# Attention of a two-block layer on one core: items head by head, value products three chunks behind, three ways out of PSUM

## The chip, the cores and the metric

The kernel runs on 1 core of a Trainium2 chip. The metric is the device time of one execution in microseconds; the time given is the median of several executions. Engines are named as in the profile: PE (TensorE matmul) and PEld (its weight loads), DVE (VectorE), ACT (ScalarE), POOL (GpSimd), SP (the queue that issues the transfers).

## The reference, cut to what matters

Two blocks are computed on 1024 tokens of width 1024, all in float32. The first block mixes gated linear attention and stick-breaking attention. The second block runs two causal attentions of 8 heads each, then a gated merge, an output projection and a feed-forward layer with a convolution. The change touches the two attentions of the second block alone:

```python
def one_block(args):                  # latent attention ("attB"), query blocks of 128
    sc = (einsum('bqhd,bshd->bhqs', qn, k_nope) + einsum('bqhd,bsd->bhqs', qr, k_rope)) * scale
    sc = where(causal, sc, -inf)
    p = softmax(sc, axis=-1)
    o = einsum('bhqs,bshd->bqhd', p, v)
...
def one_block(args):                  # indexed sparse attention ("attA"): only the 256 best keys
    ...
    sc = einsum('bqgrd,bqkgd->bqgrk', qg, ksel) * scale
    sc = where(valid, sc, -inf)
    p = softmax(sc, axis=-1)
    o = einsum('bqgrk,bqkgd->bqgrd', p, vsel)
```

In the kernel the sparse attention is computed as a dense one with a mask of the selected keys, which an earlier stage writes to DRAM.

## The kernel before, in words

Precision: a float32 operand of a matmul is split into a rounded part (`hi`, the chip's fp32r type) and a rest (`lo = x - hi`), and each product is made of two or three matmuls with these parts.

`attend` (L1576 and after) runs both attentions as one list of 64 items. A pair is two heads; there are 4 pairs of attB and then 4 of attA. An item is (pair, `tp`, `h`): one head `h` and two query tiles `t = 2*tp + w` of 128 queries, in the order `tp` = 3, 0, 2, 1, so that items have 4, 1, 3 and 2 chunks of 256 keys. Causal tiles see `(t+1)*128` keys.

- `stage_a(i, w)` makes the scores of one query tile: matmuls into one of two PSUM score tiles (`ps2`, named `pb` in the trace; L1785 to L1787 for attB, L1842 and L1843 for attA), for tiles without a mask tile one more matmul that adds the causal bias (L1630), then one DVE pass that copies the scores to an SBUF tile of the `g4` ring and takes the row minimum (L1638, or L1640 with the mask), then the exponential with its row sum on ACT (L1641). The row sums go to a small tile `l`.
- `stage_c(i, c)` transposes one chunk of 256 keys of both query tiles on PE (L217) into a PSUM tile `ps` (512 columns, 384 in the last chunk of an item; two such tiles rotate). ACT copies it to `hi` (L1657), DVE subtracts to get `lo` (L1658). Both land in SBUF tiles of the ring `pt`.
- `stage_d(i, c)` multiplies the values with `hi` and `lo` (L1674), accumulating in PSUM: `pg` for head 0, `po` for head 1.
- `finish(pair, h, bank)` follows when two items (`tp` 3 and 0, or 2 and 1) of a head are complete: ACT copies one half of the accumulator (L1687), DVE adds the other half (L1689); after head 1, the reciprocals of the row sums (L1693) are spread over a PSUM tile `ps` by matmuls (L1697), ACT copies that to SBUF (L1700) and POOL multiplies (L1701).
- `setup` runs one step of a list that prepares the next pair: transfers of queries, keys and values, transposes and splits of queries and keys (`split_T`, L1741 and L1742), splits of the values on POOL (`split_v`, L1728 and L1729).

The loop at the end of `attend` writes the work out with scores two items ahead of the products (`lag = 2`), up to two chunks transposed before the first product of the item. Not this text alone sets the order on the engines: a planner (`schedule_with_timeline_sim`, L2105) orders the instructions of every engine by a simulated timeline, with the written order as priority, and adds the waits. Each engine then runs its own queue in that order. Buffers are rings (`bufs`): a tile that is asked for waits until the oldest user of its slot is done. Before the change the stage has `g4` 8, `mb` (mask tiles) 4, `pt` 6, `r2` 3.

Of the kernel before, what the change touches and what calls it, by code (L numbers as in the profile page):

```python
# [15 lines left out]
P = 128  # L16
# [138 lines left out]
class K:  # L155
# [1434 lines left out]
    def attend(self, jobs, begun, fill):  # L1590
# [8 lines left out]
        items = [(pair, tp, h) for pair in range(4 * len(jobs)) for tp in order for h in range(2)]  # L1599
# [14 lines left out]
        def stage_a(i, w):  # L1614
# [7 lines left out]
            if h == 0:  # L1622
                live["b", pair, t] = bias(t)
# [9 lines left out]
            if (place, h, w) == (1, 0, 1):  # L1633
                live["l", pair, bank] = self.col(8, "l")
            l = live["l", pair, bank]
            j = (place * 2 + w) * 2 + h
# [12 lines left out]
        def stage_c(i, c):  # L1649
            job(items[i][0])  # L1650
            pt, n = self.ps(), 0
            for s, ws in tiles(i, c):
                for w in ws:
                    self.tr(pt[:, n:n + P], live["p", i, w][:, s * P:(s + 1) * P])
                    n += P
            hi, lo = [self.tq.tile([P, 512], F32R, tag="pt", name=self.nm("pt"), bufs=self.bufs["pt"]) for _ in range(2)]
            nc.scalar.copy(hi[:, :n], pt[:, :n])  # L1657
            nc.vector.tensor_tensor(lo[:, :n], pt[:, :n], hi[:, :n], op=OP.subtract)  # L1658
            live["pt", i, c] = hi, lo

        def stage_d(i, c):
# [3 lines left out]
            if place == 1 and c == 0:  # L1665
                live["po", h] = self.po() if h else self.pg()
            po, n = live["po", h], 0
# [12 lines left out]
        def finish(pair, h, bank):  # L1680

            oT, po = job(pair)[5], live.pop(("po", h))
            q = slice(1, 3) if bank else slice(0, 4, 3)
            o = oT[:, pair % 4].rearrange("p (q t) -> p q t", q=4)[:, q]
            hs, other = slice(64 * h, 64 * h + 64), slice(64 - 64 * h, 128 - 64 * h)
            t1 = self.r2()
            nc.scalar.copy(t1[hs], po[other])  # L1687
            q2 = lambda y: y.rearrange("p (q t) -> p q t", q=2)
            nc.vector.tensor_tensor(o[hs], q2(po)[hs], q2(t1)[hs], op=OP.add)  # L1689
            if h == 0:  # L1690
                return
            rl = self.col(8, "rl")
            nc.vector.reciprocal(rl, live.pop(("l", pair, bank)))  # L1693
            pr = self.ps()
            for j in range(8):
                hh = j % 2
                nc.tensor.matmul(pr[64 * hh:64 * hh + 64, j // 2 * P:(j // 2 + 1) * P],  # L1697
                                 rl[:, j:j + 1].to_broadcast([P, 64]), self.ident, start=True, stop=True)
            R = self.r2()
            nc.scalar.copy(R, pr)  # L1700
            nc.gpsimd.tensor_tensor(o, o, q2(R), op=OP.mult)  # L1701

        lag = 2
        for k in range(len(items) + lag):
            a, i = k < len(items), k - lag
            nch = self.nk(2 * items[i][1] + 1) // 256 if i >= 0 else 0
            if a:
                stage_a(k, 1)
            if fill:
                fill.pop(0)()  # L1710
            for c in range(min(nch, 2)):
                stage_c(i, c)
            if a:
                stage_a(k, 0)
            for c in range(nch):
                stage_d(i, c)
                if c + 2 < nch:
                    stage_c(i, c + 2)
            if k % 8 >= 1:
                setup()  # L1720

# [22 lines left out]
    def block2_b(self):  # L1744
# [4 lines left out]
        def prep(pair):  # L1749
# [11 lines left out]
            def load(h):  # L1761
                if pair and h == 0:
                    load_v()
# [13 lines left out]
            if pair == 0:  # L1777
                steps.append(load_v)
# [236 lines left out]
    def block2_front(self, first):  # L2015

        pool, causal = self.tc.tile_pool, self.causal
        with pool(name=self.nm("kp2"), bufs=1, reuse_waits="tile") as self.kp2:
# [25 lines left out]
            self.bufs = {"g4": 8, "mb": 4, "pt": 6, "r2": 3}  # L2044
# [64 lines left out]
```

## Time and profile before

| | us |
|---|---|
| median of 3 runs | 2475.01 (2467.51 to 2495.38) |
| profiled execution | 2476.42 |
| its span, first to last instruction | 2474.5 |
| PE busy in the span | 2312.6 (93%) |
| PEld busy | 1900.2 (77%) |
| DVE busy | 1452.8 (59%) |
| ACT busy | 873.0 (35%) |
| POOL busy | 884.1 (36%) |

Busy time is the time in which an engine has at least one instruction running. PE's matmuls are pipelined and their ends are modelled, so one that is shown as busy can still be behind its best pace; PEld shows the weight loads that come before every matmul. The idle time of an instruction is what its engine stood still before it, with the instruction whose end released it behind the arrow. The two attentions of the second block lie between about 1222 and 1552 us of the span.

### The profile page before, as it was taken

To read this page: it belongs to the slowest core of one execution; us is meant where nothing else is said; L and a number is where in the kernel's file an instruction comes from. 1 tells how busy PE (TensorE), PEld (TensorE's weight loads), DVE (VectorE), ACT (ScalarE), POOL (GpSimd) and SP (SyncE) were. 2 spreads that over 40 slices of the span, in tenths; PEclk is the share of its full clock that TensorE was granted. 3 is DMA by queue.
4 is the path that set the end of the run, shared out by engine and by line. 5 is a ranking of instruction groups with operands and counts; after the bars stand their busy time and mean duration, and the time that the engine had idled before them with its cause. 6 is when DMAs were issued, how large, how long until landed. Compare 5 with 4: busy or idle time off the path is not lost.

```text
span 2474.5 us, 30964 instructions
## 1 busy us (share of the span) xinstructions
PE 2312.6 (93%) x12073; PEld 1900.2 (77%) x12073; DVE 1452.8 (59%) x2189; ACT 873.0 (35%) x1389; POOL 884.1 (36%) x641
## 2 busy tenths in 40 slices
PE   4999999998798999788999998899999999999997
PEld 3788887776577888667788877788888888888886
DVE  8564457668656467999777776544433333333335
ACT  4454442443314345542376776212311111111111
POOL 5211135455466353435311010631343434443341
PEclk9999999899699999899999999999999999999999
DMA  6222122222332122344511210341111111111112
GB/s 243 98 98 100 73 90 89 79 77 91 137 111 100 65 81 101 142 111 125 161 48 39 75 34 19 119 162 35 68 43 48 47 52 52 51 52 43 52 43 79
DMA packets 116415, 206.09 MB, mean 83 GB/s; under 512 B 45458, under 2 KB 67106, under 8 KB 115874
## 3 DMA queue, kind: packets, MB, share of 16 engines
q1 hardware_dynamic: 116258, 204.01, 24.0%
q8 instruction: 97, 1.59, 0.3%
q14 instruction: 60, 0.49, 0.1%
HBM read 154.14 MB, written 49.84 MB: 82 GB/s over the span
## 4 chain that ended last, share of the span: by engine, by line
PE 43%; DVE 3%; ACT 3%; issue 1%; POOL 1%; DMA 0%; SPq 0%; POOLq 0%; DVEq 0%; ACTq 0%
PE up_pb L1935 5%; PE up_pb L1936 5%; PE up_pb L1934 5%; PE br_ps L1880 3%; PE dn_ps L1989 3%; PE dn_ps L1991 3%; PE dn_ps L1990 3%; PE dn_pb L1934 1%; PE dn_pb L1936 1%; PE dn_pb L1935 1%; PE op_ps L1087 1%; PE op_ps L1085 1%; PE op_ps L1086 1%; PE attB_ps L217 1%; PE attA_po L1674 1%
## 5 line engine op out<-in xcount | busy, mean ns | idle before, releaser
L1993 DVE TENSOR_TENSOR br_h<-br_h,dn_ps 128x512 f32<-128x512 f32 x176 | 119.6, 686 | 237.6 <-PE dn_ps L1991 237.3
L1972 DVE SCALAR_TENSOR_TENSOR ffn_ws<-up_pb,cols,ffn_ws 128x1023 f32<-128x1023 f32 x66 | 84.6, 1281 | 138.9 <-ACT ffn_ws L1970 138.1
L205 POOL TENSOR_SCALAR up_wh<-up_raw 128x1024 fp32r<-128x1024 f32 x41 | 43.6, 1063 | 272.9 <-PE up_pb L1935 134.0
L1970 ACT ACTIVATE ffn_ws<-up_pb,cols 128x1024 f32<-128x1024 f32 x33 | 40.0, 1212 | 234.9 <-PE up_pb L1936 234.9
L210 POOL TENSOR_TENSOR up_wl<-up_raw,up_wh 128x1024 fp32r<-128x1024 f32 x41 | 98.4, 2401 | 20.5 <-PE up_pb L1936 17.8
L210 POOL TENSOR_TENSOR sb_wl<-sb_raw,sb_wh 128x1024 fp32r<-128x1024 f32 x15 | 37.9, 2533 | 189.6 <-ACT sb_wh L209 189.4
L1934 PE MATMUL up_pb<-br_h,up_wh 128*128 128x512 f32 x264 | 102.7, 389 | 0.0
L1935 PE MATMUL up_pb<-br_h,up_wh 128*128 128x512 f32 x264 | 102.7, 389 | 0.0
L1936 PE MATMUL up_pb<-br_h,up_wl 128*128 128x512 f32 x264 | 102.7, 389 | 0.0
L1934 PE MATMUL up_pb<-op_fh,up_wh 128*128 128x512 f32 x264 | 102.7, 389 | 0.0
L1935 PE MATMUL up_pb<-op_fl,up_wh 128*128 128x512 f32 x264 | 102.7, 389 | 0.0
L1936 PE MATMUL up_pb<-op_fh,up_wl 128*128 128x512 f32 x264 | 102.7, 389 | 0.0
L1548 ACT ACTIVATE topk_r<-topk_r 128x640 bf16<-128x640 bf16 (+1 forms) x64 | 57.4, 898 | 120.3 <-DVE topk_r L1547 120.3
L1977 ACT CAST up_g<-ffn_ws 128x1024 fp32r<-128x1024 f32 x22 | 23.1, 1049 | 176.1 <-PE dn_ps L1990 97.7
L1989 PE MATMUL dn_ps<-dn_wh,up_g 128*128 128x512 f32 x192 | 75.2, 392 | 1.3 <-DVE br_h L1993 1.3
L1990 PE MATMUL dn_ps<-dn_wl,up_g 128*128 128x512 f32 x192 | 74.8, 389 | 0.0
L1991 PE MATMUL dn_ps<-dn_wh,up_g 128*128 128x512 f32 x192 | 74.7, 389 | 0.0
L654 PE MATMUL gla_pb<-QB,gla_X 128*128 128x128 f32 x448 | 66.7, 305 | 8.4 <-DVE QB L641 7.6
L242 PE MATMUL v_ps<-sb_wh,init_hh 128*128 128x256 f32 x256 | 74.3, 291 | 0.0
L244 PE MATMUL v_ps<-sb_wh,init_hl 128*128 128x256 f32 x256 | 74.0, 289 | 0.0
L243 PE MATMUL v_ps<-sb_wl,init_hh 128*128 128x256 f32 x256 | 73.8, 288 | 0.0
L654 PEld LDWEIGHTS gla_pb<-QB,gla_X 128*128 128x128 f32 x448 | 61.5, 214 | 12.9 <-issue 4.1
(745 smaller groups left out, 7471.9 us busy)
## 6 DMA issues: line engine op xcount, KB each, us to landing
up_raw<-in_wu SPq DMA_DIRECT2D x43, 512.0 KB, 3.4
dn_raw<-in_wu SPq DMA_DIRECT2D x21, 512.0 KB, 3.5
sb_sp<-F_st SPq DMA_DIRECT2D x32, 256.0 KB, 2.0
sb_raw<-in_wu SPq DMA_DIRECT2D x15, 512.0 KB, 4.3
init_X<-in_wada SPq DMA_DIRECT2D x13, 512.0 KB, 4.4
c_raw<-in_wu SPq DMA_DIRECT2D x13, 512.0 KB, 4.2
br_raw<-in_wu SPq DMA_DIRECT2D x12, 512.0 KB, 4.1
bq_raw<-in_wu SPq DMA_DIRECT2D x11, 512.0 KB, 3.8
```

Of the source, the lines that this page charges most:

```text
L210: (nc.gpsimd if pool else nc.vector).tensor_tensor(l, raw, h, op=OP.subtract)
L242: nc.tensor.matmul(po, hh[:, k, ts], wh[:, cs], start=(k == 0), stop=False)
L654: self.nc.tensor.matmul(pl[:, cs], X[:, cs], QB[:, cs], start=True, stop=True)
L1880: nc.tensor.matmul(po, w[:, ws], x[:, k, hs], start=(n == 0), stop=(n == 11))
L1934: nc.tensor.matmul(o, wh[:, s], self.hh[h][:, kk], start=(kk == 0), stop=False)
L1935: nc.tensor.matmul(o, wh[:, s], self.hl[h][:, kk], start=False, stop=False)
L1936: nc.tensor.matmul(o, wl[:, s], self.hh[h][:, kk], start=False, stop=(kk == KT - 1))
L1972: nc.vector.scalar_tensor_tensor(u[:, d:], p[:, :T - d], tap(2 - d), u[:, d:], op0=OP.mult, op1=OP.add)
L1989: nc.tensor.matmul(po, hi[:, ts], wh[:, cs], start=(k == 0), stop=False)
L1990: nc.tensor.matmul(po, hi[:, ts], wl[:, cs], start=False, stop=False)
L1991: nc.tensor.matmul(po, lo[:, ts], wh[:, cs], start=False, stop=(k == 1))
L1993: nc.vector.tensor_tensor(x, x, po, op=OP.add)
```

## The change

The order of the items changes from two heads side by side to head after head. The scores stay two items ahead, but the loop now runs over chunks: after the transposes of a chunk come the value products of the chunk three before it, and the two score tiles of the item two ahead are put at the start and in the middle of an item. The accumulator is `pg` or `po` by the half of the query tiles, not by the head. The transposed chunk leaves PSUM in one of three ways, by `(i + c) % 3`: as before; or copied as float32 by ACT, or by DVE, into a tile of the ring `r2`, from which POOL makes `hi` and `lo`. `finish` is complete for each head (four reciprocals and products each, on 64 partitions) where it was for both heads together. Masks are loaded for each head. The load and split of the values is the last step of every pair's preparation. The rings are `g4` 7, `mb` 4, `pt` 8, `r2` 4.

```diff
@@ -1596,7 +1596,7 @@
         nc = self.nc
 
         order = (3, 0, 2, 1)
-        items = [(pair, tp, h) for pair in range(4 * len(jobs)) for tp in order for h in range(2)]
+        items = [(pair, tp, h) for pair in range(4 * len(jobs)) for h in range(2) for tp in order]
         states, live = {}, {}
         states[0], todo = begun
 
@@ -1619,8 +1619,7 @@
                 todo.extend(steps)
             t = 2 * tp + w
             _, _, score, bias, _, _ = job(pair)
-            if h == 0:
-                live["b", pair, t] = bias(t)
+            live["b", pair, t] = bias(t)
             n = self.nk(t)
             off, chunks = self.key_chunks(n)
             z = self.ps2()[:, off:]
@@ -1630,10 +1629,10 @@
                 nc.tensor.matmul(z[:, n - P:n], self.idb, self.cb[:, t], start=False, stop=True, skip_group_check=True)
             place, bank = {0: 0, 3: 1, 1: 0, 2: 1}[tp], tp in order[2:]
             p, mn = self.g4(), self.col(1, "mn")
-            if (place, h, w) == (1, 0, 1):
-                live["l", pair, bank] = self.col(8, "l")
-            l = live["l", pair, bank]
-            j = (place * 2 + w) * 2 + h
+            if (place, w) == (1, 1):
+                live["l", pair, h, bank] = self.col(4, "l")
+            l = live["l", pair, h, bank]
+            j = place * 2 + w
             if b is None:
                 nc.vector.tensor_scalar(p[:, :n], z[:, :n], 1.0, None, op0=OP.mult, op1=OP.min, accum_out=mn)
             else:
@@ -1653,9 +1652,16 @@
                 for w in ws:
                     self.tr(pt[:, n:n + P], live["p", i, w][:, s * P:(s + 1) * P])
                     n += P
-            hi, lo = [self.tq.tile([P, 512], F32R, tag="pt", name=self.nm("pt"), bufs=self.bufs["pt"]) for _ in range(2)]
-            nc.scalar.copy(hi[:, :n], pt[:, :n])
-            nc.vector.tensor_tensor(lo[:, :n], pt[:, :n], hi[:, :n], op=OP.subtract)
+            hi, lo = [self.tq.tile([P, 512], F32R, tag="pt", name=self.nm("pt"), bufs=self.bufs["pt"])[:, :n] for _ in range(2)]
+            way = (i + c) % 3
+            if way == 0:
+                nc.scalar.copy(hi, pt[:, :n])
+                nc.vector.tensor_tensor(lo, pt[:, :n], hi, op=OP.subtract)
+            else:
+                x = self.r2()[:, :n]
+                (nc.scalar.copy if way == 1 else nc.vector.tensor_copy)(x, pt[:, :n])
+                nc.gpsimd.tensor_scalar(hi, x, 1.0, 0.0, op0=OP.mult, op1=OP.add)
+                nc.gpsimd.tensor_tensor(lo, x, hi, op=OP.subtract)
             live["pt", i, c] = hi, lo
 
         def stage_d(i, c):
@@ -1663,8 +1669,8 @@
             _, _, _, _, v, _ = job(pair)
             place, bank = {0: 0, 3: 1, 1: 0, 2: 1}[tp], tp in order[2:]
             if place == 1 and c == 0:
-                live["po", h] = self.po() if h else self.pg()
-            po, n = live["po", h], 0
+                live["po"] = self.po() if bank else self.pg()
+            po, n = live["po"], 0
             end = self.nk(2 * tp + 1) // P - 1
             x = live.pop(("pt", i, c))
             for s, ws in tiles(i, c):
@@ -1679,45 +1685,46 @@
 
         def finish(pair, h, bank):
 
-            oT, po = job(pair)[5], live.pop(("po", h))
+            oT, po = job(pair)[5], live.pop("po")
             q = slice(1, 3) if bank else slice(0, 4, 3)
-            o = oT[:, pair % 4].rearrange("p (q t) -> p q t", q=4)[:, q]
             hs, other = slice(64 * h, 64 * h + 64), slice(64 - 64 * h, 128 - 64 * h)
-            t1 = self.r2()
+            o = oT[hs, pair % 4].rearrange("p (q t) -> p q t", q=4)[:, q]
+            t1, R = self.r2(), self.r2()
             nc.scalar.copy(t1[hs], po[other])
-            q2 = lambda y: y.rearrange("p (q t) -> p q t", q=2)
-            nc.vector.tensor_tensor(o[hs], q2(po)[hs], q2(t1)[hs], op=OP.add)
-            if h == 0:
-                return
-            rl = self.col(8, "rl")
-            nc.vector.reciprocal(rl, live.pop(("l", pair, bank)))
+            q2 = lambda y: y[hs].rearrange("p (q t) -> p q t", q=2)
+            nc.vector.tensor_tensor(o, q2(po), q2(t1), op=OP.add)
+            rl = self.col(4, "rl")
+            nc.vector.reciprocal(rl, live.pop(("l", pair, h, bank)))
             pr = self.ps()
-            for j in range(8):
-                hh = j % 2
-                nc.tensor.matmul(pr[64 * hh:64 * hh + 64, j // 2 * P:(j // 2 + 1) * P],
-                                 rl[:, j:j + 1].to_broadcast([P, 64]), self.ident, start=True, stop=True)
-            R = self.r2()
-            nc.scalar.copy(R, pr)
+            for j in range(4):
+                nc.tensor.matmul(pr[hs, j * P:(j + 1) * P], rl[:, j:j + 1].to_broadcast([P, 64]), self.ident,
+                                 start=True, stop=True)
+            nc.scalar.copy(R[hs], pr[hs])
             nc.gpsimd.tensor_tensor(o, o, q2(R), op=OP.mult)
 
-        lag = 2
-        for k in range(len(items) + lag):
-            a, i = k < len(items), k - lag
-            nch = self.nk(2 * items[i][1] + 1) // 256 if i >= 0 else 0
-            if a:
-                stage_a(k, 1)
+
+        for i in range(2):
+            for w in (1, 0):
+                stage_a(i, w)
             if fill:
                 fill.pop(0)()
-            for c in range(min(nch, 2)):
+        behind = []
+        for i, (pair, tp, h) in enumerate(items):
+            nch = self.nk(2 * tp + 1) // 256
+            for c in range(nch):
+                if i + 2 < len(items):
+                    if c == 0:
+                        stage_a(i + 2, 1)
+                    if c == nch // 2:
+                        stage_a(i + 2, 0)
                 stage_c(i, c)
-            if a:
-                stage_a(k, 0)
-            for c in range(nch):
-                stage_d(i, c)
-                if c + 2 < nch:
-                    stage_c(i, c + 2)
-            if k % 8 >= 1:
+                behind.append((i, c))
+                if len(behind) > 3:
+                    stage_d(*behind.pop(0))
+            if i % 8:
                 setup()
+        for x in behind:
+            stage_d(*x)
 
     def r2(self):
         return self.tq.tile([P, 512], F32, tag="r2", name=self.nm("r2"), bufs=self.bufs["r2"])
@@ -1759,8 +1766,6 @@
                 self.split_v(v[0], r.rearrange("p (n d) -> p n d", d=64))
 
             def load(h):
-                if pair and h == 0:
-                    load_v()
                 f = self.slot16("F", F32R).rearrange("p (j t) -> p j t", j=4)
 
                 raw = []
@@ -1774,8 +1779,7 @@
             for h in range(2):
                 for j in range(2):
                     steps.append(lambda h=h, j=j: self.split_T(F[h][1][j], 96, F[h][0][:, 2 * j], F[h][0][:, 2 * j + 1]))
-            if pair == 0:
-                steps.append(load_v)
+            steps.append(load_v)
             return (F, v), steps
 
         def score(st, h, t, z, chunks):
@@ -2041,7 +2045,7 @@
                     self.nc.sync.dma_start(self.dbg["mask"], self.maskd)
             if self.stop == "topk":
                 return
-            self.bufs = {"g4": 8, "mb": 4, "pt": 6, "r2": 3}
+            self.bufs = {"g4": 7, "mb": 4, "pt": 8, "r2": 4}
             with pool(name=self.nm("tq3"), bufs=1, reuse_waits="tile") as self.tq:
                 self.attend([job_b, self.block2_a()], (state, steps[6:]),
                             self.gate_halves("gA7", lambda: self.g4()[:, :512]))
```

## Rows read from the trace of the kernel before

**Rows 1.** Stages: length; PE, PEld, DVE, ACT, POOL busy; clock, DMA share.
```profile
1222.00:1404.00 182.00, 173.24 (x1262) 149.06 (x1263) 132.23 (x271) 131.51 (x270) 22.56 (x16) 0.97 0.22 63
1404.00:1552.00 148.00, 129.94 (x948) 110.13 (x946) 104.09 (x221) 104.90 (x224) 12.73 (x11) 1.00 0.12 35
...
1222.00:1552.00 330.00, 303.18 (x2208) 259.19 (x2208) 236.32 (x491) 236.41 (x493) 35.29 (x27) 0.98 0.18 51
```

**Rows 2.** Waits of PE's loads, 1222 to 1552: us, times, longest; value products.
```profile
PEld attA_po L1674 <- DVE attA_pt L1658: 7.1, 18, 1.5
PEld attA_pg L1674 <- DVE attA_pt L1658: 4.9, 11, 0.5
PEld attB_pg L1674 <- DVE attB_pt L1658: 2.2, 6, 0.5
PEld attB_pg L1674 <- ACT attB_pt L1657: 1.8, 4, 0.8
PEld attA_po L1674 <- ACT attA_pt L1657: 1.7, 6, 0.4
PEld attA_pg L1674 <- ACT attA_pt L1657: 1.5, 5, 0.5
PEld attB_po L1674 <- DVE attB_pt L1658: 1.3, 3, 0.8
PEld attB_po L1674 <- ACT attB_pt L1657: 1.2, 5, 0.3
```

**Rows 3.** The same view: score products and transposes that wait for a bank.
```profile
PEld attA_pb L1842 <- DVE attA_c L1640: 7.5, 14, 1.0
PEld attA_ps L217 <- ACT attA_r L1700: 5.9, 5, 1.7
PEld attB_pb L1785 <- DVE attB_g L1638: 2.7, 5, 0.9
PEld attB_ps L217 <- ACT attB_r L1700: 2.0, 2, 1.8
```

**Rows 4.** PE in order of time: start, duration, instruction.
```profile
1414.99 0.44 PE L1842 MATMUL attA_pb<-attT_ks,attT_F 128*128 128x384 f32 x1
1415.27 0.34 PE L1843 MATMUL attA_pb<-attT_ks,attT_F 128*128 128x384 f32 x1
```

**Rows 5.** Groups on ACT by shape: busy us, mean ns, idle before and releaser.
```profile
L1657 ACT CAST attB_pt<-attB_ps 128x512 fp32r<-128x512 f32 x48 | 27.9, 583 | 15.7 <-PE attB_ps L217 15.0 <-DVE attA_c L1640 0.6
...
L1700 ACT COPY attA_r<-attA_ps 128x512 f32<-128x512 f32 x8 | 4.7, 586 | 0.2
```

**Rows 6.** Instructions of line 1657: shortest, median, longest ns; first and last start.
```profile
L1657 ACT CAST attB_pt<-attB_ps x80: 456/573/619, 1234.5 to 1399.5; 128x512 fp32r<-128x512 f32 x48, 128x384 fp32r<-128x384 f32 x32
```

**Rows 7.** Groups on DVE, with columns as in rows 5; L876 lies in the first block.
```profile
L1658 DVE TENSOR_TENSOR attA_pt<-attA_ps,attA_pt 128x512 fp32r<-128x512 f32 x48 | 32.9, 689 | 17.5 <-ACT attA_pt L1657 17.3
L1658 DVE TENSOR_TENSOR attA_pt<-attA_ps,attA_pt 128x384 fp32r<-128x384 f32 x32 | 17.6, 552 | 1.5 <-ACT attA_pt L1657 1.5
L876 DVE COPY sb_tmp<-sb_pg 128x512 f32<-128x512 f32 x24 | 16.5, 686 | 33.9 <-PE sb_pg L217 33.8
L1693 DVE RECIPROCAL attA_c<-attA_c 128x8 f32<-128x8 f32 x8 | 1.6, 199 | 3.6 <-ACT attA_g L1641 3.6
```

**Rows 8.** Instructions of three lines on POOL, with columns as in rows 6.
```profile
L1728 POOL TENSOR_SCALAR attT_ks<-attT_g x2: 625/796/966, 1360.5 to 1436.8; 128x512 fp32r<-128x512 f32 x2
L1701 POOL TENSOR_TENSOR attT_oA<-attT_oA,attA_r x8: 1267/1274/1292, 1422.5 to 1551.7; 128x512 f32<-128x512 f32 x8
L1863 POOL TENSOR_TENSOR br_ol<-topk_oB,br_oh x4: 1717/1740/1757, 1553.0 to 1558.1; 128x512 fp32r<-128x512 f32 x4
```

**Rows 9.** POOL in order of time, around a value split, with its idle time.
```profile
1236.81 1.04 POOL L1728 TENSOR_SCALAR attT_vhl<-attT_g 128x1024 fp32r<-128x1024 f32 x1 [13.31 <-DMA attT_g<-x_vBd]
```

**Rows 10.** Transfers from 1255 to 1325: issues, KB each, us to landing.
```profile
attT_g<-x_vBd SPq DMA_DIRECT2D x2, 512.0 KB, 3.8
```

## The prediction

> **What bounds the kernel now.** The page comes first: over the whole span PE is the busiest engine, and the slices from about the 20th to the 25th are the attentions of the second block. Only they are changed, so the second view is the busy time of each engine there, 1222 to 1552 us [rows 1]. PE is busy 303 of 330 us, its weight loads 259, DVE 236, ACT 236, POOL 35. PE is not the whole story: DVE and ACT stand at 72% in the first half of the stage (first attention, to 1404) and at 70 to 71% in the second, although PE's load falls from 95% to 88%. That is the picture of three engines that hand small tiles to each other and wait in turn, with POOL nearly free.
>
> The third view is the waits of PE's weight loads. The value products wait for the split tiles of the transposed weights: 15.5 us for the DVE half of the pair and 6.2 us for the ACT half, 21.7 us in 58 waits [rows 2]. Score products wait for a score bank that DVE has not emptied, 10.2 us, and transposes for the bank that a finish has filled, 7.9 us [rows 3]. So 39.8 us are waits of kinds that the change touches. A wait costs a little more than itself: a score product of 384 columns behind one took 0.44 us, the next one, whose load was early, 0.34 [rows 4]; 58 such steps of 0.10 are an estimate of 6 us more.
>
> How much could be won at all? By PE's own busy time the stage has 330 - 303 = 27 us to give, by its loads 330 - 259 = 71 [rows 1]. I take the second as the ceiling, since the waits of rows 2 and 3 alone are more than 27.
> The Trainium skill, Perfetto Trace Analysis, section Identifying the Most-Contended Engine, says the same of headroom in general: matmul busy time misleads because matmuls are pipelined, and weight-load busy time is to be used. With the first ceiling the best possible time would be some 2449 us, with the second some 2405; the trace agrees with the second, by the 39.8 us of named waits.
>
> **The change, part by part.** *Three ways out of PSUM.* Counting the new rule over the 160 chunks gives 54 of way 0 (as before), 54 of way 1 (ACT copies, POOL splits) and 52 of way 2 (DVE copies, POOL splits); of the 106 POOL chunks 63 have 512 columns and 43 have 384.
> ACT loses 52 copies (32 x 0.583, the 20 narrow ones at an estimated 0.47: 28 us) and gains 16 copies of 0.586 in the finishes (9 us) [rows 5]: 236 becomes 217.
> DVE loses 106 subtracts (63 x 0.689 + 43 x 0.552 = 67 us), gains 52 copies (32 x 0.686, 20 at an estimated 0.55: 33 us) and 16 reciprocals of 0.2 (3 us) [rows 7]: 236 becomes 206. None of this lies on the path; it matters because DVE stands in order behind ACT: it sat 18.8 us waiting for ACT's half in the second attention alone [rows 7], with the score passes queued behind it. Two thirds of these ordered waits go.
> POOL gains a pair per chunk: 0.625 + 1.27 us for 512 columns, plus an estimated 0.07 between, so 1.97; three quarters of it, 1.48, for 384 [rows 8]. 63 x 1.97 + 43 x 1.48 = 188 us. The finish multiplies double from 16 to 32, though of half the partitions; I price each as the full one, 1.27 (half of it would be the lower bound): 41 us. With some 15 us of value and key splits POOL comes to 244 us, the second-busiest engine after PE.
>
> *Value products three chunks behind.* A chunk lasts 330/160 = 2.06 us now, so three are 6.2 us; at the floor of 259 us they are 4.9. A lone POOL chunk needs 0.58 + 1.97 = 2.6 us from its last transpose. The longest runs of POOL chunks are five (way 1 and 2 alternating across items): the fifth ends 0.58 + 5 x 1.97 = 10.4 us after the first transpose, and its product is due 4 chunks later plus the three, 7 x 1.7 = 11.9 us at a pace of 1.7. So the lag covers the latency, with 1.5 us left, unless a finish multiply (1.27) falls into the run: then nothing is left. Of the 21.7 us I take 19 as gone, and the 6 behind them; bounds are 0 (POOL takes the place of DVE as the one waited for) and 28. For late POOL tiles I add 3.
> *Score waits.* Two items ahead as before; DVE has 30 us less to do and fewer ordered waits. Of 10.2 I take 8 (bounds 0 and 10).
> *Finishes.* PE's sixteen small products per pair of heads stay the same in number, but there are 32 finishes with a PSUM tile each, and the copy of it stands on ACT behind the copy that waits for the last value product. Rows 3 show 7 waits of 7.9 us for 16 finishes; 32 could make it 16. The accumulator, in return, alternates by half of the queries, so that a new item never needs the bank just finished. I take +4 (bounds -4 and +8).
> *Moved and doubled transfers.* The value load is now the last step of a pair, not the first: one transfer on SP, no longer ahead of the query and key loads, and two POOL instructions. POOL sat 13.3 us for such a load [rows 9], then free; now chunk splits stand behind it. A load lands in 3.8 us [rows 10], so a split queued right behind the issue holds POOL some 4 us, which the lag just covers: +2 over three pairs and two key loads (bounds 0 and 12). The 24 mask loads become 48, issued two items (five chunks on average, some 10 us) ahead of their use: nothing; if the four mask buffers did bind, DVE's score pass would wait for a landing, an estimated 1 us in each of 24. One score buffer fewer (7) still holds three items' six and one spare: nothing, save at the two key loads, which take two.
>
> Sum: -19 - 6 - 8 + 3 + 4 + 2 = -24 us. As a cross-check, ACT and DVE set the pace at 72%: with 8% and 13% less on them, 330 would fall to about 303, -27. I take -25. The profiled execution took 2476.4 us, 1.4 above the median of 2475.0, so 2450 us from the median. The ceiling per half agrees: the second half has POOL at about 120 of its 148 us, so it can hardly give more than 15.
>
> **Rivals.** *A, the forecast*, stage about 305 us: 2435 to 2460. For it: the lag, longer than every latency in the rows. Against: the planner, not the text, sets the order on PE, and may pull products forward again. Chance 0.50.
> *B, POOL takes over as the one waited for.* POOL's queue is in order; a multiply of a finish waits for two copies and a sum, a value split for its transfer, and chunk splits stand behind both, while ACT's copies wait for one of four small tiles that POOL frees late. It decides when POOL needs more than some 90% of a stretch: the second half. Then only the score waits and a third of the product waits are won, 8 + 9, less 6 to 20: -11 to +3, 2464 to 2478. The same time results if the executed order keeps the old distance. Chance 0.23.
> *C, slower: POOL and DVE slow each other.* In the branches right after, the same 128x512 subtract took POOL 1.740 us beside DVE subtracts, and a scalar step beside a DVE subtract took 0.966 and not 0.625 [rows 8]. At these prices the pair is 2.7 us (384: 2.0): 63 x 2.7 + 43 x 2.0 + 32 x 1.74 + 15 = 327 us. POOL can start only when the first chunk is out, 13 us into the stage (the first copy is at 1234.5 [rows 6]): 340 us, and with half a microsecond of ordered waiting in each of 32 finishes 356: 2501. The point is a mean POOL subtract above 1.5 us. Against it: the finish multiplies in this stage took 1.27 beside a DVE at 72% [rows 1, 8], whose instructions here read PSUM and at most one tile of SBUF; in the branches both operands lie in SBUF. Chance 0.13.
> The Trainium skill has both sides. Perfetto Trace Analysis, section Optimizing Scalar/DVE Operations, warns that moving work between DVE and GpSimd might not help, as they share a read port; SBUF - State Buffer, section Who interferes with whom, limits this to DVE instructions with two SBUF inputs or in a two-port mode. The rows agree with the narrower rule (1.27 here, 1.74 in the branches).
> *D, more*: PE reaches its loads' floor within 20 us, stage about 280: 2425. Needs all waits of rows 2 and 3 and most unnamed ones gone. Chance 0.14.
>
> **The numbers.** About 1% (25 us) is what a measurement of this kernel can tell from no change. A puts 0.34 beyond that and 0.16 within; D is faster (0.14); B is within (0.21) save 0.02 slower; C gives 0.11 slower and 0.02 within. Faster 0.48, same 0.39, slower 0.13. The likeliest case alone would be 2435 to 2460; the range 2424 to 2479 leaves out half of D and most of C, and takes in B and the bounds of products, scores and finishes.
>
> **What would show it.** In the changed profile: product waits on split tiles under 5 us, and where there are any, on POOL; DVE near 206, ACT near 217, POOL near 244 us with subtracts near 1.28 us at 512 columns; score waits down by most; bank waits behind finishes between 4 and 16; the stage near 305 us and all else the same within 2 us. I am wrong if POOL's subtracts take over 1.5 us, if product waits on POOL exceed 15 us, or if the pace of the first attention (PE-heavier) does not fall too.

## The result, and the profile after

The changed kernel takes 2458.91 us (median of 20 runs, 2450.84 to 2472.31), the kernel before 2476.65 (20 runs beside them): a ratio of 0.9933 with a 95% interval of 0.9914 to 0.9951, which is 16.6 us less, from 12 to 21. The forecast was 2450, 25 us less.

The span of the profiled execution is 2449.0 us, 25.5 less than before; that is more than the change. The last projection product ahead of the attentions starts at 1218.73 before and at 1207.09 after, 11.64 us apart, although nothing is changed there (one cause is in the trace: from 428 to 446 us the granted clock was 0.53 in the execution before, near the lower of TensorE's two levels, and 1.00 in the one after). So I compare stages, not spans. The stage is taken from the first score product to the first product of the branches, the stage that follows: 329.2 us before (1222.81 to 1552.04), 317.7 after, and 316.2 in a repeat of the change.

The stage view of the changed kernel, both attentions, then the whole; columns as in rows 1:

```profile
1207.32:1384.50 177.18, 171.28 (x1255) 151.49 (x1253) 113.53 (x243) 121.96 (x248) 130.46 (x136) 0.98 0.25 71
1384.50:1525.02 140.52, 132.09 (x957) 115.53 (x956) 91.67 (x205) 98.34 (x210) 112.30 (x122) 1.00 0.21 62
1207.32:1525.02 317.70, 303.37 (x2209) 267.02 (x2208) 205.20 (x448) 220.30 (x457) 242.76 (x257) 0.99 0.23 67
```

Against [rows 1] DVE has lost 31 us, ACT 16, POOL has gained 207. PE's busy time is the same, 303, but its weight loads have grown from 259 to 267, which the prediction had not expected.

The largest waits of PE's loads on split tiles, on score banks and on PSUM tiles (us, times, longest), as in [rows 2, 3]:

```profile
PEld attA_pg L1680 <- POOL attA_pt L1664: 2.4, 7, 0.7
PEld attB_ps L217 <- ACT attB_r L1702: 2.2, 2, 1.2
PEld attA_ps L1700 <- ACT attA_r L1662: 1.9, 4, 0.5
PEld attA_ps L217 <- ACT attA_r L1662: 1.9, 2, 1.3
PEld attB_pb L1789 <- DVE attB_g L1637: 1.8, 4, 0.7
PEld attA_pb L1846 <- DVE attA_c L1639: 1.4, 5, 0.4
...
PEld attA_pg L1680 <- ACT attA_pt L1658: 1.0, 1, 1.0
...
PEld attA_po L1680 <- POOL attA_pt L1664: 0.7, 3, 0.3
...
PEld attA_po L1680 <- POOL attA_pt L1663: 0.5, 2, 0.3
```

Where 21.7 us of product waits stood in [rows 2], 4.6 are left in these rows (5.0 with two of 0.2 on POOL that are not shown), and most of that is on POOL now. The score waits of [rows 3], 10.2, are 3.2.

POOL's groups by shape (busy us, mean ns, idle before and releaser), answering to [rows 8]:

```profile
L1664 POOL TENSOR_TENSOR attA_pt<-attA_r,attA_pt 128x512 fp32r<-128x512 f32 x32 | 41.0, 1281 | 2.5
...
L1703 POOL TENSOR_TENSOR topk_oB<-topk_oB,attB_r 64x512 f32<-64x512 f32 x16 | 20.5, 1281 | 10.2 <-ACT attB_r L1702 6.8 <-DVE topk_oB L1695 3.0
```

The subtract takes 1.281 us, as forecast, and the finish multiply takes as long on 64 partitions as it did on 128: taking the full price was right.

Last, the spreading products of line 1700 (the row sums' reciprocals), first by group and then one finish in order of time:

```profile
L1700 PEld LDWEIGHTS attA_ps<-idr,attA_c 128*64 128x64 f32 x128 | 13.5, 136 | 3.4 <-ACT attA_r L1662 1.9 <-issue 0.2
L1700 PEld LDWEIGHTS attB_ps<-idr,attB_c 128*64 128x64 f32 x128 | 13.5, 136 | 2.1 <-issue 0.5 <-DVE attB_r L1662 0.2
```

```profile
1394.18 0.85 PEld L1700 LDWEIGHTS attA_ps<-idr,attA_c 128*64 128x64 f32 x8
```

And the same in the kernel before, where the line is 1697 (rows that the prediction left out):

```profile
L1697 PEld LDWEIGHTS attB_ps<-idr,attB_c 128*64 128x64 f32 x128 | 6.8, 136 | 0.8
L1697 PEld LDWEIGHTS attA_ps<-idr,attA_c 128*64 128x64 f32 x128 | 6.8, 136 | 0.8
```

```profile
1417.53 0.85 PEld L1697 LDWEIGHTS attA_ps<-idr,attA_c 128*64 128x64 f32 x16
```

256 loads of 136 ns each in both kernels (a float32 product stands as two instructions), but before they kept PE's loading busy for 13.6 us and now for 27.0. Sixteen loads took 0.85 us when they went by turns into the two halves, the lower and the upper 64 partitions of the PSUM tile; eight take the same 0.85 us now that a finish sends all of them into one half. The mean of one instruction does not show this, the busy time of the group does.

### The profile page after: what moved, and what is told of

Its sections match the earlier page's. It is cut to its first block, busy times and chain, and to the rows that moved or that the text cites. A ratio compares the mean times of both kernels' runs of the same rounds, so it can differ in the third digit from the quotient of the medians.

```text
span 2449.0 us, 31277 instructions
## 1 busy us (share of the span) xinstructions
PE 2310.1 (94%) x12073; PEld 1909.1 (78%) x12073; DVE 1421.7 (58%) x2151; ACT 856.2 (35%) x1353; POOL 1087.2 (44%) x869
## 4 chain that ended last, share of the span: by engine, by line
PE 54%; DVE 10%; ACT 1%; POOL 1%; issue 1%; DMA 0%; DVEq 0%; POOLq 0%; ACTq 0%; SPq 0%
PE up_pb L1940 5%; PE up_pb L1939 5%; PE up_pb L1938 5%; DVE topk_jk L1550 4%; PE br_ps L1884 3%; PE dn_ps L1993 3%; PE dn_ps L1995 3%; PE dn_ps L1994 3%; DVE topk_r L1547 2%; PE dn_pb L1938 1%; PE dn_pb L1940 1%; PE dn_pb L1939 1%; PE c_ps L242 1%; PE attB_ps L217 1%; PE c_ps L244 1%; PE c_ps L243 1%
## 5 line engine op out<-in xcount | busy, mean ns | idle before, releaser
L210 POOL TENSOR_TENSOR up_wl<-up_raw,up_wh 128x1024 fp32r<-128x1024 f32 x41 | 98.5, 2403 | 20.2 <-PE up_pb L1940 17.5
```

Source lines behind the costliest of these rows:

```text
L210: (nc.gpsimd if pool else nc.vector).tensor_tensor(l, raw, h, op=OP.subtract)
```

## The experiments

Every run is put on one scale with the stage as defined above, taken apart as loads (PEld busy), waits (the rows of the wait view that name a tile, added up, the wait ahead of the first branch product included; the pause ahead of the first score, 4.1 us in the kernels that have it, is not counted) and the rest, in which the loads of the bias product stand with 6.3 to 7.7 us of waits that name no tile. Two profiles of the same attentions differ by 1.5 us or less (317.7 and 316.2; 329.2 twice). The ratios are to the kernel before, run on the same chip.

| kernel | median us | ratio, 95% | stage | loads | waits | rest |
|---|---|---|---|---|---|---|
| before | 2476.65 | | 329.2 | 259.2 | 48.5 | 21.5 |
| the change | 2458.91 | 0.9933 (0.9914 to 0.9951) | 317.7 | 267.0 | 29.7 | 21.0 |
| the change, repeated | 2460.57 | 0.9924 (0.9899 to 0.9949) | 316.2 | 265.7 | 29.9 | 20.6 |
| before, products by half | 2484.37 | 1.0026 (0.9998 to 1.0055) | 335.7 | 266.9 | 45.5 | 23.3 |
| the change, joint finish | 2436.73 | 0.9826 (0.9801 to 0.9852) | 296.5 | 252.4 | 24.1 | 20.0 |
| joint finish, products by half | 2441.86 | 0.9860 (0.9823 to 0.9898) | 302.2 | 260.0 | 22.3 | 19.9 |
| the change, products by turns | 2452.49 | 0.9908 (0.9876 to 0.9939) | 309.1 | 252.7 | 32.8 | 23.6 |
| the change, one way | 2464.22 | 0.9958 (0.9927 to 0.9989) | 326.6 | 269.4 | 37.0 | 20.2 |
| one way, joint finish | 2449.79 | 0.9884 (0.9851 to 0.9918) | 304.5 | 251.9 | 32.8 | 19.8 |
| one way, joint finish, lag 1 | 2461.49 | 0.9938 (0.9916 to 0.9959) | 318.0 | 256.4 | 41.2 | 20.4 |
| before with three ways | 2481.02 | 1.0008 (0.9977 to 1.0039) | 335.1 | 260.3 | 53.2 | 21.6 |
| the change, lag 1 | 2481.46 | 1.0018 (0.9992 to 1.0044) | 342.5 | 269.6 | 52.7 | 20.2 |
| before, test of positions late | 2478.14 | 0.9997 (0.9975 to 1.0019) | 329.2 | 258.9 | 48.1 | 22.2 |

The rest moves by less than 4 us: what makes a stage longer or shorter here is mostly its loads and its named waits.

The granted clock is not the same in all of these stages. It was at half, the lower of the two levels, for 10.2 us of the stage before, 6.8 of the change, 3.4 of its repeat, 17.4 of "before with three ways" and none of "one way, joint finish"; the other kernels had 3.4 to 6.8, and "before, products by half" 10.2. Half of these times is a bound for what the clock cost (an estimate: PE at half speed all the while). The two stages of 329.2 us had 10.2 and 6.8 and the same length. The differences below are not corrected for it.

The theory from the two profiles: the lag and the ways won what was forecast, and the finish per head took some 13 us of it back, because its products go into one half. Rivals: POOL, late in its queue; the finish as such (more tiles, copies and multiplies); the planner, which need not keep the written distance; the clock, which fell twice right behind the attentions in the profile of the change.

**The change, repeated.** No edit.

> The change as it is, again, beside the others on one chip. Both theories: about 17 us under the kernel before (2455 to 2464 when before is at 2476). Theory 'one half': the 8 spreading products of each finish start 0.12 to 0.13 us apart, the weight loads of that line (L1700) are busy 27 us in all where before they were 13.6. Rival 'clock': the granted clock falls twice behind the attentions again, as in the first profile (3.4 and 6.8 us at 1.2 GHz), and that costs some 4 us of the gain.

It gave 0.9924 and a stage of 316.2, with 27.0 us of spreading loads again, 0.11 us apart: the first reading holds. The clock did fall twice behind the attentions, for 3.4 us each, and from the first branch product to the end the kernel took 922.2 us, where the kernel before, whose clock did not fall there, took 922.4. So the rival of the clock does not explain a loss.

**Before, products by half.** The products in the order of their halves, at the old number of finishes:

```diff
-            for j in range(8):
+            for j in (0, 2, 4, 6, 1, 3, 5, 7):
```

> The kernel before with one thing changed: the 16 spreading products of a finish are issued head by head (8 into partitions 0 to 63, then 8 into 64 to 127) and not alternating. Same instructions, same data. Theory 'one half': their weight loads take 27 us of PE instead of 13.6; before had 71 us of idle PE loads, so not all of it shows: 5 to 13 us slower, 2481 to 2489 where before is at 2476. Rivals: no difference (0 to 2 us).

The spreading loads of the second attention in this kernel:

```profile
L1697 PEld LDWEIGHTS attA_ps<-idr,attA_c 128*64 128x64 f32 x128 | 10.7, 136 | 0.8
```

The loads of the group went from 13.6 to 21.4 us (this row and its twin for attB), the stage from 329.2 to 335.7; the total, 1.0026, is not resolved. Sixteen in this order take 1.34 us (a row below), between 0.85 and twice that, so the half that comes next already overlaps. The order alone costs loads, with nothing else changed.

**The change, joint finish.** The normalization once for both heads, as in the kernel before; all else as in the change (the diff is cut):

```diff
+            if h == 0:
+                return
...
             for j in range(4):
-                nc.tensor.matmul(pr[hs, j * P:(j + 1) * P], ...)
-            nc.scalar.copy(R[hs], pr[hs])
+                for hh in range(2):
+                    nc.tensor.matmul(pr[64 * hh:64 * hh + 64, j * P:(j + 1) * P], ...)
+            R = self.r2()
+            nc.scalar.copy(R, pr)
...
```

> The change with the second half of the finish done once for both heads, as before the change: 16 spreading products that alternate between the two halves of the output partitions, one copy, one POOL multiply of 128 partitions. Theory 'one half' (products into the same 64 partitions one after the other cost 0.13 us each, alternating ones 0.06): PE has 13 us less to do, so 8 to 13 us under the change, some 2445 to 2452 where the change is at 2459. Rival 'POOL is what is late': POOL loses 16 multiplies (20 us of 243) and ACT 16 copies; product waits on POOL are only 3.8 us in the trace, so at most 4 us. Rival 'clock': no change, 2459.

The stage of that kernel, columns as in rows 1, and one finish:

```profile
1214.38:1510.91 296.53, 284.13 (x2210) 252.39 (x2208) 203.53 (x448) 209.52 (x441) 221.94 (x241) 0.99 0.28 75
```

```profile
1408.13 0.85 PEld L1704 LDWEIGHTS attA_ps<-idr,attA_c 128*64 128x64 f32 x16
```

This is the fastest kernel of the case: 0.9826, 23.8 us under the repeat of the change on the same chip. That is more than the 8 to 13 us expected. The stage is 20 to 21 us shorter, more than the 13.4 us of loads: the loads fall by 14.6, the waits by 5.6, with 16 copies on ACT and 16 multiplies on POOL fewer (ACT from 220 to 210, POOL from 243 to 222 us). Which of the two carries the gain, the half or the fewer tiles, copies and multiplies, was left open by this run; the next two tell.

**The change, products by turns.** Finishes stay per head; two of the four products go into the other half of the PSUM tile, and a second ACT copy brings them back (the diff is cut):

```diff
-                nc.tensor.matmul(pr[hs, j * P:(j + 1) * P], ...)
-            nc.scalar.copy(R[hs], pr[hs])
+                nc.tensor.matmul(pr[other if j % 2 else hs, ...], ...)
+            for y in range(2):
+                nc.scalar.copy(R[hs]..., pr[other if y else hs]...)
```

> The change, but the four spreading products of a finish go alternately into the two halves of the partitions of their PSUM tile, and two ACT copies of 256 columns bring them together; number of products, finishes, PSUM tiles and POOL multiplies as in the change. If it is the half that makes the products dear (theory): their loads fall from 27.0 us to about 13.5, the stage from 317 us by 13 less what 32 more ACT copies cost (at most 8), so 304 to 312, 2446 to 2455 us. If the joint finish gained by fewer tiles, copies and multiplies alone (rival): loads or not, the stage stays at 317 or grows by up to 8: 2459 to 2467.

One finish of this kernel:

```profile
1404.30 0.42 PEld L1700 LDWEIGHTS attA_ps<-idr,attA_c 128*64 128x64 f32 x8
```

Eight loads take 0.42 us instead of 0.85 with nothing else done to them. Loads fall by 14.3 us and the stage by 7.1 to 8.6, inside the range of the theory and outside the rival's; 3 us come back as waits (products wait 10.5 us for split tiles, 5.0 in the change, with 32 more ACT copies) and 3 as rest. The total, 0.9908, does not by itself differ from the change's.

**Joint finish, products by half.** The same from the other side:

```diff
-            for j in range(4):
-                for hh in range(2):
+            for hh in range(2):
+                for j in range(4):
```

> The joint finish, with its sixteen products of a pair and half in the order of the halves (eight and then eight, well, four and four) and not alternating; all else as in the joint finish. If the half alone makes the price: the loads of these products go from 13.6 us to some 21, as in the kernel before with grouped products, and the stage from 296.5 to about 303: 2443 us. If the joint finish gained by fewer tiles, copies and multiplies: 2437, within 3.

```profile
1420.48 1.34 PEld L1704 LDWEIGHTS attA_ps<-idr,attA_c 128*64 128x64 f32 x16
```

Loads up by 7.6, the stage up by 5.7 (296.5 to 302.2), as the theory had it; the totals, 0.9860 and 0.9826, overlap. So a microsecond of these loads costs about three quarters of one in the stage, and of the 20 us of the joint finish some 10 are the half (an estimate, 0.75 x 13.4; two profiles of one kernel differ by up to 1.5 us). The other 10 are left for all that comes once per finish, the tiles, copies and multiplies, by difference and not by a run of their own.

**The change, one way.** Order, lag and finishes of the change; every chunk leaves by ACT and DVE:

```diff
-            way = (i + c) % 3
+            way = 0
```

> The change with way 0 alone: every chunk leaves PSUM by ACT and DVE as before, so POOL has only the finishes and splits; order of items, three chunks of lag, finishes per head and rings as in the change. If the lag alone removes the product waits (19 of 21.7 us), this keeps most of the gain: some 2460 to 2466. If the relief of ACT (236 to 217 us) and DVE (236 to 206) carries the gain, it is near the kernel before, 2470 to 2480 (ACT comes to 245 us, DVE to 239, and the 13 us of dearer products are not paid for).

326.6 us: the ways are worth 9 to 10 us of stage on top of order and lag. The total, 2464.22, lies where the lag alone was to put it, but the stage is only 2.6 us under the kernel before, since its loads are 10 us more. The product waits are gone in this kernel too (5.2 us), so order and lag, not POOL, remove them; the ways take the score waits (9.3 here, 3.9 in the change).

**One way, joint finish.** The same edit on the joint kernel, so that order and lag stand alone, at the old price of the finishes:

```diff
-            way = (i + c) % 3
+            way = 0
```

> Order of the items and distance of three chunks as in the change, one way out of PSUM (ACT and DVE, as before), the finish joint for both heads: the order and the lag at the old price of the finishes. If the terms add (theory): the way-0 kernel had a stage of 326.6, the joint finish takes some 15 to 20 off, so 307 to 312, 2444 to 2452 us. If the dear finish was hidden there behind the waits for DVE and ACT (rival): the stage stays at 320 to 327, 2457 to 2464.

```profile
1217.64:1522.15 304.51, 289.66 (x2210) 251.94 (x2208) 231.06 (x503) 234.87 (x493) 39.32 (x29) 1.00 0.27 74
```

The terms add, and a little more than expected: 304.5, with DVE, ACT and POOL about as busy as before. Order and lag, with the rings and all else of the new loop, are worth 24.7 us of stage; the ways 8.0 more (296.5).

**One way, joint finish, lag 1.**

```diff
-                if len(behind) > 3:
+                if len(behind) > 1:
```

> Head by head, joint finish, one way out of PSUM, value products one chunk behind and not three: against the same with three this is the lag alone, against the kernel before the order of the items with a lag. If the distance is the gain: the stage goes from 304.5 to 320 to 332, 2466 to 2480 us. If the order of the items (an item of few chunks no longer beside one of the same length) is the gain: it stays at 304 to 312, 2449 to 2457.

```profile
1217.24:1535.25 318.01, 298.14 (x2210) 256.38 (x2208) 234.09 (x503) 237.13 (x493) 39.56 (x29) 0.99 0.26 70
```

318.0, between the two expectations: neither was right alone. The lag is worth 13.5 us. The order of the items with a lag of one, and with it the rings and all else of the new loop, is worth 11.2; no run parts these. Product waits are 22.3 us with a lag of one, as before the change, and 4.2 with three. The largest of them with one, and behind them the largest with three:

```profile
PEld attA_pg L1680 <- DVE attA_pt L1659: 5.3, 11, 0.6
PEld attA_po L1680 <- ACT attA_pt L1658: 4.8, 13, 0.7
PEld attA_po L1680 <- DVE attA_pt L1659: 3.4, 9, 0.5
```

```profile
PEld attB_po L1680 <- ACT attB_pt L1658: 1.4, 4, 0.5
PEld attA_po L1680 <- ACT attA_pt L1658: 1.2, 4, 0.5
```

Of the waits, what the order takes away with a lag of one is that of transposes for a PSUM tile, 7.9 before and 1.1 here; with a lag of three it is back (10.2), two thirds of it for DVE's subtracts of chunks in place of the copies of finishes.

**The change, lag 1.** The same edit on the change itself (`> 3` becomes `> 1`).

> The change with the value products one chunk behind and not three. If the written distance sets the order on PE: a POOL tile needs 2.6 us alone and up to 10 in a run of five, a chunk lasts 2.0 us, so product waits on POOL rise from some 4 us to 20 to 40, the stage from 317 to 330 to 345: 2470 to 2487. If the planner sets the order whatever the text's distance: 2456 to 2463.

The size was right (342.5, ratio 1.0018), so the written distance does set the order. The place was not: product waits came to 10.5 us only, and transposes waited 20.2, mostly for the copies of finishes and chunks:

```profile
PEld attA_ps L217 <- ACT attA_r L1702: 7.1, 8, 1.4
PEld attB_ps L217 <- ACT attB_r L1702: 3.8, 5, 1.2
PEld attA_ps L217 <- ACT attA_r L1662: 3.2, 7, 1.1
PEld attA_po L1680 <- POOL attA_pt L1664: 3.0, 5, 0.9
```

**Before with three ways.** The ways and the rings on the kernel before, in the old order and distance:

```diff
+            way = (i + c) % 3
...
+                (nc.scalar.copy if way == 1 else nc.vector.tensor_copy)(x, pt[:, :n])
+                nc.gpsimd.tensor_scalar(hi, x, 1.0, 0.0, op0=OP.mult, op1=OP.add)
+                nc.gpsimd.tensor_tensor(lo, x, hi, op=OP.subtract)
...
-            self.bufs = {"g4": 8, "mb": 4, "pt": 6, "r2": 3}
+            self.bufs = {"g4": 7, "mb": 4, "pt": 8, "r2": 4}
```

> The kernel before with the three ways out of PSUM and the rings of the change but six more tiles none (g4 7, pt 8, r2 4), in the old order of items and with the old distance of products. If the lag is what covers POOL's latency: product waits on POOL take the place of those on DVE, 15 to 35 us, and the stage stays at 330, from 325 to 340: 2470 to 2485. If the ways gain by the work taken off DVE and ACT, lag or no lag: score and product waits fall by some 15, stage 315 to 320, 2460 to 2467.

335.1 and 1.0008: DVE 31 us and ACT 24 us less busy than before, and nothing gained. Product waits (18.2) have moved to POOL, and the waits of transposes have grown from 7.9 to 20.7:

```profile
PEld attA_po L1681 <- POOL attA_pt L1665: 7.8, 9, 1.2
PEld attA_ps L217 <- ACT attA_r L1707: 4.5, 6, 1.1
PEld attA_ps L217 <- ACT attA_r L1663: 3.7, 7, 0.8
```

**Before, test of positions late.** Every kernel in the new order, and the one before with three ways, also lost a pause of 4 us ahead of the first score. Before, DVE's queue held a cast that waited 9.67 us for a small transfer (`fpos`, for a test of the positions, L291), and the split of the keys, for which PE waits, stood behind it:

```profile
1220.54 0.58 DVE L294 CAST fposf<-fpos 8x128 f32<-8x128 int32 x1 [9.67 <-DMA fpos<-in_posr]
...
1221.56 2.33 DVE L1742 TENSOR_TENSOR attT_F<-attT_pb,attT_F 96x1024 fp32r<-96x1024 f32 x2
```

```profile
1222.81 0.19 PEld L1785 LDWEIGHTS attB_pb<-attT_F 96*128 96x128 f32 x1 [4.11 <-DVE attT_F L1742]
```

In the changed kernel the planner put the cast behind the attentions (1536.71). The experiment does that alone, on the kernel before:

```diff
-        with self.tc.tile_pool(name="fp", bufs=1, reuse_waits="tile") as kp:
+        for kp in (self.tq,):
```

> The kernel before with one edit outside the attentions: the small tiles of the test of the positions (L291 to L301) come from the pool of the feed-forward stage, so that their transfer and cast are ordered behind the attentions; the attentions are untouched. If the wait of DVE for that transfer is what held PE between the last projection product and the first score (theory): the pause of 4.1 us there becomes 0.2, the stage itself stays at 329 within 2, 2472 us against 2476. If another thing held PE there (the split of the keys itself, a transfer of the queries), the pause stays at 3 to 4 us and the time at 2476.

The pause is gone in the trace (0.2 us; the load of the first score has no wait any more), and the stage behind it is the same 329.2. The total is 0.9997, from 6 us less to 5 more: too wide to show 4 us or to exclude them. In the ten other kernels without the pause the total fell by 3 to 10 us more than the stage, 6 on average (the change: 16.6 against 11.5), which speaks for a gain outside the stage; this run by itself does not. What the other 2 us are, no run shows. How much of the measured 16.6 us is the pause stays open between 0 and 4.

## Why the prediction was right, and what it missed

**What held, and what was luck.** The range, 2424 to 2479, is 55 us wide and takes in no change at all, so that it held says little. The likeliest case, 2435 to 2460, holds by 1 us, and with help from outside: the stage, the only part that the forecast changed, fell by 11.5 to 13.0 us to 317.7, half of the 25 that were forecast, and not to the 305 named as a sign; the other 5 of the 16.6 us lie outside it. The outcome held likeliest, a gain of more than 1% (0.48), did not come: it is 0.7%, with an interval to 0.9. The signs inside the stage held: product waits 5.0 us and on POOL, DVE 205, ACT 220, POOL 243 us, subtracts of 1.281 us. So did the pace of the first attention, from the first score to the first transposes of the second: 179.8 us before, 173.4 after.

**Product waits.** -19 and +3 for late POOL tiles was -16; measured 22.2 to 5.0 us with the small releasers, -17.2, and what is left is on POOL. The lag-1 run with one way shows that it is the lag: product waits of 22.3 with one chunk, 4.2 with three.

**Knock-on, -6.** In part: all loads but the spreading ones fell by 5.6 us, and 3.6 of it are the loads of the value products, 94.6 us before and 91.0 after. Over the runs these go with the product waits: 94.6 to 96.2 us where the waits are 21 to 22 (three runs in the old order, and the new one with one way and a lag of one), 89.7 to 91.9 where they are 4 to 6, and 91.1 to 92.8 between. That is a reading across runs; none changes it alone. The rest fell by 0.5 to 0.9 us; the granted clock in the stage was 0.98 before and 0.99 after.

**Score waits, -8.** The two kinds named went from 10.2 to 3.2, -7; one-way against three-way shows that this is what the ways are for.

**Finishes' banks, +4.** Transposes and spreading products waited 7.9 us for PSUM tiles before and 10.3 now, +2.4. As waits for a bank this is inside the bounds of -4 and +8. As the price of a finish per head it is not: the runs with and without the joint finish put that at +20.5 us.

**Transfers, +2.** No load of PE in the changed stage waits for a transfer, and POOL's largest wait for one is 1.1 us: nothing.

**The step that failed** is the sentence "PE's sixteen small products per pair of heads stay the same in number". The number is the same, 256 loads of 136 ns; their price is not. I took the term at nothing, by count, where the group's busy time, 6.8 us for 128 loads of 136 ns each (17.4 if they stood one behind another), was in the trace and said that they overlapped. Missed: 13.4 us of loads, of which some 10 reach the stage, and some 10 more for the doubled tiles, copies and multiplies, which the sum left off the path.
The Trainium skill, TensorEngine Tiling (Array Packing), section Tiling Modes, has the rule under its key properties: different tiles of the array can load and multiply in parallel; its list of configurations has 128x64 as two tiles. The trace agrees, with 16 loads in 0.85 us by turns and 8 in 0.85 within one half.
A second term, smaller, had no place in the sum: loads that waited for nothing visible, 1.9 us before and 7.8 after, +5.9. The longest of them, 2.0 us, stands ahead of the first value product of the stage, which itself waited 1.85 us for ACT's half; it is a product wait, then, at the start of the lag.

The stage's sum, as measured by its waits and loads: waits 48.5 to 29.7 (-18.8: products -17.2, scores -9.1 with all releasers, tiles +2.4, issue +5.9, others -0.8), loads +7.8 (spreading +13.4, others -5.6), rest -0.5; -11.5 us, and -13.0 in the repeat. With 0 to 4 us of the pause that is 11.5 to 17, against 12 to 21 from the runs.

By experiments instead of waits: order of items with the rest of the loop -11.2, lag -13.5, ways -8.0, finish per head +20.5 (296.5 to the mean of 317.7 and 316.2), sum -12.2. Against the terms of the sum, the lag's -22 (-19, -6, +3) came to -13.5, the ways' -8 to -8.0, the finish's +4 to +20.5, the transfers' +2 to nothing; the order of the items had no term, and its 11 us made up for part of what the finish and the lag fell short. Had the finish stayed joint, the forecast of -25 would have been too small.

**The rivals.** B, POOL as the one waited for, does not hold: 4 us. It does hold in the old order, where products wait 15 us for POOL and the ways win nothing. With the ways and a lag of one these waits are 9 us, and more of the loss stands at the transposes. The distance is its condition. C does not hold: subtracts of 1.281 us, not 1.5. D did not come true, but the joint kernel at 2436.73 goes half the way from the forecast to it: the ceiling by loads was the right one to look at, since 296.5 is already below the 303 us of PE's busy time in [rows 1].

## What to carry to other kernels

When small products that fill half of the array are regrouped, look at the group's busy time and not at count times duration: if it is far below that product (here 0.39 of it, 0.78 in one half), they overlap, and an order that sends them into one half can raise their price; here it doubled it. A hand-over that is moved to a freer but slower engine paid here only behind enough distance: three ways in the old loop won nothing, the new order and lag without the ways 24.7 us of stage. And price a tail step that is split in two at all its parts, the PSUM tile, the copy and the multiply: here it gave back 20 of 33 us.

## What the runs showed of the hardware

Loads of 128x64 into the two halves ran side by side: 16 by turns took 0.85 us, 8 by turns 0.42. Into one half 8 took 0.85, one every 0.11 us, so that loads of 0.136 us overlapped by little; 16 in two groups by half took 1.34. A multiply of 64 partitions x 512 columns took POOL 1.281 us, as one of 128 partitions did [rows 8]. Right behind the attentions the granted clock differed though the work is the same: 0.76 over the first 21 us of the branches in the changed kernel, 1.00 before; from the first branch product to the end the changed kernel took 924.0 us and the one before 922.4, a difference of 1.6.

```profile
1525.00:1546.00 21.00, 17.20 (x52) 12.68 (x53) 15.86 (x19) 8.40 (x16) 15.85 (x11) 0.76 0.28 101
```
